# Feed forwards in passes of 8, 8 and 6 inner tiles, with the down projections by seven products of quarters

## The chip, the cores and the metric

The kernel runs on one core of a Trainium2 chip. The metric is the time of one execution in device microseconds; the figure for a kernel is the median of several executions. The engines of the core that matter here are TensorE (PE, with its weight loads as PEld), VectorE (DVE), ScalarE (ACT), GpSimd (POOL) and SyncE (SP); SP issues most of the transfers, and POOL issues those that add to what lies in the target. In this kernel each engine has one stream of instructions, whose order is fixed when the kernel is built.

## The reference, cut to what matters

A trunk of two layers for 512 tokens of width 1024, in f32. Layer 0 mixes with a gated delta rule, layer 1 with sliding window attention; both also attend to 256 memory tokens. Behind the mixer stands in each layer the feed forward, with an inner width of 2816:

```python
def swiglu(h, w_gate_up, w_down):
    gu = h @ w_gate_up
    return (jax.nn.silu(gu[..., :D_FF]) * gu[..., D_FF:]) @ w_down
...
        x = x + jnp.concatenate([mix_out.astype(x.dtype), mem_o.astype(x.dtype)], axis=-1) @ w_out[layer]
        x = x + swiglu(rms_norm(x, ln_ffn[layer]), w_gate_up[layer], w_down[layer])
...
    return rms_norm(x, ln_final)
```

Layer 1 rotates queries and keys by tables of cosines and sines of the positions (the rope tables).

## The kernel before

Activations lie transposed: a tile holds 128 features by 512 tokens, so the residual x is 8 tiles and the inner layer is 22. Every product runs as three matmuls (`mm3`): each operand is split into a high part, a copy by ACT (names `whi`, `h`, `Tah`), and a low part, a subtraction by DVE (`wlo`, `l`, `Tal`), and high by high, high by low and low by high are added up in PSUM. So every weight and every activation costs one ACT copy and one DVE subtraction (`split`, L168). Weights come from memory by SP's transfers into `wraw` and `ws`.

The feed forward (`ffn`, L1099) runs in two halves of 11 inner tiles each: first the gate and up projections of the half, then the half's share of all 8 rows of the down projection. Of the gate and up projections, a few are direct (8 weight tiles by three matmuls, 512 tokens wide, in the PSUM tiles `pj`). The rest go in pairs of output tiles by `quarters` (L1275): the input is cut in two halves of features and two of tokens, the weights of the pair likewise, and seven products of quarters replace the eight of the plain way, as in Strassen's method. Each product is 4 weight tiles by three matmuls, 256 tokens wide, in the PSUM tiles `g`. Sums of weights are made by POOL's accumulating transfers into `ws` and by DVE in `wraw`; sums of the input's quarters (`token_sums`) are made once in a layer. DVE joins the products from PSUM (`fu`, `fg`), and three of them are held for it by ACT copies (`fs`). Six places for split weights (`ring`) go round.

The down projections are direct: for each of 8 rows 11 weight tiles, split as pieces 768 and 640 wide, by three matmuls of 512 tokens. In layer 1 the last two rows run in halves of the tokens, so that the final norm and the store of the first half begin before the second half is done. Behind the first down row of layer 0 stands `rope_tables`: two tens of small DVE steps that depend on each other, all on one tile `ws` and one tile `fu`, with two sines on ACT. Behind layer 0's feed forward the next layer (`swa`) splits x twice by two gains, once for its queries and once for keys and values (`h`, `l` from `x`), and then projects the queries.

The order on each engine comes from the framework's scheduler, which sets the instructions by the order in the code, by priorities and by its own estimates of when operands are there; the code adds a few ordering edges (`nosync`).

Of the kernel before, what the change touches and what calls it, by code (L numbers as in the profile page):

```python
# [9 lines left out]
F32 = mybir.dt.float32  # L10
F32R = mybir.dt.float32r
# [7 lines left out]
P = 128  # L19
# [67 lines left out]
class Builder:  # L87
# [158 lines left out]
    def build(self):  # L246
        tc, nc, a = self.tc, self.nc, self.a
        with ExitStack() as st:
            opened = lambda name, **kw: tc.tile_pool(name=name, bufs=1, reuse_waits="tile", **kw)
            pool = lambda name, **kw: st.enter_context(opened(name, **kw))  # L250
            cp = pool("const")
            self.wpool, self.apool = pool("w"), pool("acta")
            self.dpool = pool("scratch", space=DRAM)
            self.load_constants(cp)
            self.weng = nc.vector
            with opened("layer0", side="right") as self.mpool:
                with self.banks(pj=3, g=2, sc=3):
                    with opened("early", side="right") as ep:
                        self.mem_and_norm(ep)
                    with opened("gdn", side="right") as gp:  # L260
                        mix = self.gdn(gp)
                    self.bpool, xp = pool("actb"), pool("x")
                    self.x = [self.t(xp, [P, T], F32, f"x{k}") for k in range(KD)]
                    for k in range(KD):
                        nc.sync.dma_start(self.x[k], a["xT"][:, k, :])
                    self.rstd, self.cosT, self.sinT = (self.t(xp, [P, T], F32, n) for n in ("rstd", "cosT", "sinT"))
                    h = self.output(xp, 0, mix)
            with opened("ffn0", side="right") as fp, self.banks(pj=2, g=6):
                self.ffn(fp, xp, 0, h, self.apool, rope=True)
            with self.banks(pj=2, qk=2, pt=2), opened("swa", side="right") as sp:  # L270
                h = self.output(xp, 1, *self.swa(sp))
            with opened("ffn1", side="right") as fp, self.banks(pj=2, g=6):
                self.ffn(fp, xp, 1, h, self.bpool)
# [825 lines left out]
    def ffn(self, fp, xp, layer, h, apool, rope=False):  # L1099
# [3 lines left out]
        half = FT // 2  # L1103
        acts, sums, open_pairs, places, waiting, shift, sized = [], [], [], [], [], [0], []

        col = lambda f, up: a["wgu"][layer, 2 * f + up]

        def gate(f, up=()):
            ps = self.project(col(f, 0), h, "pj")
            if f == 0:  # L1110
                list(zip(range(2), up))
                self.rstd_from(acc, *(self.t(fp, [P, T], F32R, "ws", 4) for _ in range(2)), after=self.last,
                               root=(self.cosT, self.sinT) if layer else None)
                self.use(SILU_SIN)
            g = self.t(fp, [P, T], F32, "fg", 4)
            self.tt(nc.vector, g, ps, self.rstd, ALU.mult)
            if f == 2:
                waiting.append(g)
            else:
                self.fn(g, g, AF.Silu)  # L1120
            return g

        def put(u):
            n = len(acts)
            if n == FT // 2 - 1 and not sized:
                sized.append(self.t(fp, [P, 40], F32, "rest"))
            acts.append(self.pair(apool) if n < KD else self.pair(fp, f"ac{n}"))
            self.split(u, *acts[-1])
# [10 lines left out]
        def begin(f, up, by, tag, bufs, then):  # L1139

            o = [self.t(fp, [P, T], F32, tag, bufs) for _ in range(2)]
            steps = self.quarters(fp, [col(f + i, up) for i in range(2)], sums, by, o, ring)
            shift[0] = P - 8
            next(steps)
            while waiting:
                x = waiting.pop()
                self.nosync(self.fn(x, x, AF.Silu), self.held)
            end()
            next(steps)
            open_pairs.append((steps, then, o))  # L1150
            return o

        def end():
            if open_pairs:
                steps, then, o = open_pairs.pop()
                next(steps, None)
                for x in o:
                    then(x)

        def add(x, ps):  # L1160
            d = ps
            if not layer:
                d = self.t(fp, [P, T], F32, "fu", 3)
                self.tt(nc.vector, d, ps, self.rstd, ALU.mult)
            self.tt(nc.vector, x, d, x, ALU.add)

        for f0 in (0, half):
            acts.clear()
            places.clear()
            up = self.projected(col(f0, 1), h, "g")  # L1170
            g = gate(f0, up)
            u = self.t(fp, [P, T], F32, "fu", 3)
            self.tt(nc.vector, u, list(up)[-1], g, ALU.mult)
            put(u)
            for f in range(f0 + 1, f0 + half, 2):
                if f == 1:
                    g = []
                    for i in range(2):
                        for _ in range(2 - i):
                            sums.append(self.token_sums(fp, layer, len(sums), h))  # L1180
                        g.append(gate(f + i))
                    sums.append(self.token_sums(fp, layer, len(sums), h))
                else:
                    g = begin(f, 0, (self.rstd, self.rstd), "fg", 4, lambda x: self.fn(x, x, AF.Silu))
                begin(f, 1, g, "fu", 3, put)
            end()
            self.acc = self.floor if layer else None
            tail = KD - 2 if f0 and layer else KD
            down = lambda m, j, n, **kw: self.weight(a["wdn"][layer, m][:, (f0 + j) * P:(f0 + j + n) * P], **kw)
            for m in range(tail):  # L1190
                if layer and f0 == 0:
                    self.tt(nc.vector, self.x[m], self.x[m], self.root, ALU.mult)
                ps = self.bank("pj")
                for j, n in ((0, 6), (6, 5)):
                    w = down(m, j, n)
                    for k in range(n):
                        self.mm3(ps, w, k, acts[j + k], j + k == 0, j + k == half - 1)
                add(self.x[m], ps)
                if f0:
                    self.acc = self.accumulate(xp, self.acc, self.x[m], m)  # L1200
                if rope and f0 == 0 and m == 0:
                    self.rope_tables(fp)
        if tail < KD:

            parts = (slice(0, T // 2), slice(T // 2, T))
            own = dict(pool=fp, tags=("T", "T"), bufs=8)
            w = {m: [down(m, j, n, **(own if m == KD - 1 else {})) for j, n in ((0, 6), (6, 5))] for m in range(tail, KD)}
# [5 lines left out]
            for t in parts:  # L1213
                acc = self.acc[:, t]
                for m in range(tail, KD):
# [4 lines left out]
                    for k in range(half):  # L1220
                        act = [part[:, t] for part in acts[k]]
                        self.mm3(ps, w[m][k // 6], k % 6, act, k == 0 and not seeded, k == half - 1, seeded)
                    if seeded:
                        x = ps
                    else:
                        add(x, ps)
# [8 lines left out]
            for n, (end, o) in enumerate(zip(ends, outs)):  # L1235
                self.store(*end, o, n)
# [9 lines left out]
    def token_sums(self, fp, layer, j, h):  # L1246
# [9 lines left out]
        c = self.t(fp, [P, q], F32, "fc")  # L1256
        raws = [self.t(fp, [P, T], F32, f"ac{8 + j % 3}{n}") for n in "hl"]
# [17 lines left out]
    def quarters(self, fp, src, sums, by, u, ring):  # L1275
# [3 lines left out]
        (a11, a12), (a21, a22) = ([c[:, :T], c[:, T:]] for c in src)  # L1279
        a1 = self.load(src[0])  # L1280
        s1, s3 = (self.t(fp, [P, T], F32, "ws", 4) for _ in range(2))
# [6 lines left out]
        last = self.t(fp, [P, T], F32, "wraw", 2)  # L1288
# [5 lines left out]
        def product(ps, raw, b, first):  # L1294

            w = ring()
            self.split(raw, *w)
            for j in range(4):
                self.mm3(ps, w, j, sums[j][b], first and j == 0, j == 3, not first)
# [6 lines left out]
        product(pa, a1[:, :T], "11", True)  # L1306
# [6 lines left out]
        self.tt(nc.vector, a1[:, :T], s1, a1[:, :T], ALU.add)  # L1313
        product(pa, a1[:, :T], "t2", False)
        u2 = held(pa)
        product(pb, a1[:, T:], "21", True)
        self.tt(nc.vector, u[0][:, :q], pb, p1, ALU.add)
        self.tt(nc.vector, a1[:, T:], a1[:, :T], a1[:, T:], ALU.add)
        product(pc, a1[:, T:], "22", False)
        self.tt(nc.vector, u[0][:, q:], pc, u2, ALU.add)  # L1320
        self.tt(nc.vector, u[0], u[0], by[0], ALU.mult)
        product(pa, s3, "t3", False)
        self.stt(u[1][:, q:], pa, -1.0, p5, ALU.mult, ALU.subtract)
        self.tt(nc.vector, u[1][:, q:], u[1][:, q:], by[1][:, q:], ALU.mult)
        yield
        product(pa, last, "t4", False)
        self.stt(u[1][:, :q], pa, -1.0, by[1][:, :q], ALU.mult, ALU.mult)
# [227 lines left out]
def layout(i):  # L1555
# [25 lines left out]
    gu = f("w_gate_up")  # L1581
    pair = [j for t in range(FT) for j in (t, FT + t)]
# [3 lines left out]
    for k in range(0, KD, 2):  # L1586
# [10 lines left out]
        "wdn": np.stack([tiles(w) for w in f("w_down")]),  # L1597
# [20 lines left out]
```

## Time and profile before

| what | value |
|---|---|
| time, median of 3 executions | 1130.86 us (1130.72 to 1131.07) |
| the profiled execution: span from first to last instruction | 1129.4 us |
| mean granted TensorE clock of the profiled execution | 0.998 |
| PE busy | 1119.9 us, 99% of the span |
| PEld busy | 986.1 us, 87% |
| DVE busy | 827.6 us, 73% |
| ACT busy | 634.4 us, 56% |
| POOL busy | 73.2 us, 6% |
| mean traffic | 134 GB/s |

The profiled execution is known by its span alone; the median lies 1.5 us above it, which is what stands around the first and the last instruction. The table reads so: the engine with the largest share is PE, and the chain of work that ended last runs through it. The busy share of DVE is a mean over stages of different kinds and has to be read stage by stage.

### The profile page before, as it was taken

Reading aid. Unit: us, or ns where it says so; the run is one execution under the profiler, and the core shown is the slowest. Engines: PE = TensorE matmul, PEld = TensorE weight load, DVE = VectorE, ACT = ScalarE, POOL = GpSimd, SP = SyncE. Lnnn points to the kernel's source line nnn. Section 1 sums busy time; section 2 is a strip of 40 time slices with the busy share of each in tenths; the row PEclk is TensorE's granted clock in tenths of the full one; section 3 lists DMA queues with packets and bytes.
Section 4 is the critical chain, followed back from the end, with each engine's and each line's share of the span. In section 5 each row is a group of like instructions: output and inputs, shape, how many; then the busy total and the mean of one; then the engine's idle time right before and its main releaser. Section 6 shows DMA issues by size and latency. Waiting matters only on the chain.

```text
span 1129.4 us, 19330 instructions
## 1 busy us (share of the span) xinstructions
PE 1119.9 (99%) x7339; PEld 986.1 (87%) x7339; DVE 827.6 (73%) x1553; ACT 634.4 (56%) x1285; POOL 73.2 (6%) x91
## 2 busy tenths in 40 slices
PE   9999999999999999999999999999999999999997
PEld 8888778887899988899988887788999988999986
DVE  7676976577888975588955877839999634889643
ACT  8588664456566632366643555856666422666434
POOL 0000000000021001011000000000111000111001
PEclk9999999999999999999999999999999999999999
DMA  8344252234567536377533321116687533776232
GB/s 314 109 153 149 95 131 86 85 113 145 174 167 195 143 111 169 102 191 195 134 89 102 132 75 38 53 43 180 158 201 185 144 103 105 173 190 156 77 103 87
DMA packets 72401, 151.15 MB, mean 134 GB/s; under 512 B 16956, under 2 KB 18516, under 8 KB 72308
## 3 DMA queue, kind: packets, MB, share of 16 engines
q1 hardware_dynamic: 60884, 129.21, 36.3%
q0 software_dynamic: 11136, 20.45, 11.2%
q8 instruction: 57, 0.93, 0.3%
q14 instruction: 36, 0.29, 0.1%
q10 hardware_dynamic: 288, 0.26, 0.1%
HBM read 142.94 MB, written 6.96 MB: 133 GB/s over the span
## 4 chain that ended last, share of the span: by engine, by line
PE 96%; DVE 2%; ACT 1%; DMA 0%; issue 0%; DVEq 0%; SPq 0%; ACTq 0%
PE pj L146 46%; PE g L146 38%; PE sc L146 6%; PE qk L146 3%; PE pt L146 2%; PE pt L150 1%; PE g L150 1%; DVE big L153 1%; DVE qv L156 0%; DVE btmp L153 0%; DMA early<-in_early 0%; DVE wlo L153 0%; ACT sm L134 0%; DVE T L153 0%; DVE gcr L153 0%
## 5 line engine op out<-in xcount | busy, mean ns | idle before, releaser
L140 ACT ACTIVATE whi<-wraw 128x512 fp32r<-128x512 f32 (+3 forms) x318 | 235.3, 748 | 240.6 <-PE pj L146 164.0
L153 DVE TENSOR_TENSOR wlo<-wraw,whi 128x512 fp32r<-128x512 f32 (+3 forms) x318 | 262.8, 837 | 92.7 <-ACT whi L140 85.2
L146 PE MATMUL pj<-h,whi 128*128 128x512 f32 (+1 forms) x652 | 256.4, 395 | 0.0
L146 PE MATMUL pj<-l,whi 128*128 128x512 f32 (+1 forms) x652 | 254.4, 390 | 0.0
L146 PE MATMUL pj<-h,wlo 128*128 128x512 f32 (+1 forms) x652 | 254.0, 390 | 0.0
L146 PE MATMUL g<-T,whi 128*128 128x256 f32 x1216 | 216.8, 279 | 0.0
L146 PEld LDWEIGHTS g<-T,whi 128*128 128x128 f32 x1216 | 185.1, 188 | 1.3 <-DVE fu L156 1.3
L146 PE MATMUL g<-T,wlo 128*128 128x256 f32 x608 | 169.7, 279 | 0.0
L146 PEld LDWEIGHTS pj<-h,whi 128*128 128x128 f32 x652 | 122.4, 188 | 28.0 <-issue 4.1
L146 PEld LDWEIGHTS pj<-h,wlo 128*128 128x128 f32 x652 | 122.5, 188 | 25.4 <-issue 0.9
L146 PE MATMUL g<-l,whi 128*128 128x256 f32 (+1 forms) x500 | 144.5, 289 | 0.0
L146 PE MATMUL g<-h,whi 128*128 128x256 f32 (+1 forms) x500 | 144.4, 289 | 0.0
L146 PE MATMUL g<-h,wlo 128*128 128x256 f32 (+1 forms) x500 | 144.4, 289 | 0.0
L146 PEld LDWEIGHTS pj<-l,whi 128*128 128x128 f32 x652 | 122.6, 188 | 23.6 <-DVE l L1468 0.3
L146 PEld LDWEIGHTS g<-T,wlo 128*128 128x128 f32 x608 | 114.3, 188 | 0.0
L146 PEld LDWEIGHTS g<-h,whi 128*128 128x128 f32 x500 | 94.0, 188 | 1.9
L146 PEld LDWEIGHTS g<-l,whi 128*128 128x128 f32 x500 | 93.9, 188 | 1.9
L146 PEld LDWEIGHTS g<-h,wlo 128*128 128x128 f32 x500 | 93.9, 188 | 1.8
L1286 POOL DMA_DIRECT2D ws<-in_wgu x38 | 33.5, 881 | 733.0 <-DMA ws<-in_wgu 399.1
L140 ACT ACTIVATE whi<-ws 128x512 fp32r<-128x512 f32 x76 | 48.0, 631 | 42.0 <-PE g L146 35.6
L153 DVE TENSOR_TENSOR wlo<-ws,whi 128x512 fp32r<-128x512 f32 x76 | 52.0, 684 | 5.9 <-ACT whi L140 5.9
L1287 POOL DMA_DIRECT2D ws<-in_wgu x38 | 34.2, 900 | 196.4 <-DVE wlo L153 71.4
(421 smaller groups left out, 1683.2 us busy)
## 6 DMA issues: line engine op xcount, KB each, us to landing
wraw<-in_wgu SPq DMA_DIRECT2D x50, 512.0 KB, 4.4
ws<-in_wgu SPq DMA_DIRECT2D x76, 256.0 KB, 3.4
ws<-in_wgu POOLq DMA_DIRECT2D x76, 256.0 KB, 4.5
wraw<-in_win SPq DMA_DIRECT2D x26, 512.0 KB, 3.6
wraw<-in_wdn SPq DMA_DIRECT2D x32, 384.0 KB, 3.1
wraw<-in_wdn SPq DMA_DIRECT2D x32, 320.0 KB, 2.9
wraw<-in_wgu SPq DMA_DIRECT2D x38, 256.0 KB, 4.0
wraw<-in_wout SPq DMA_DIRECT2D x16, 512.0 KB, 3.6
```

The costliest lines, as they stand in the source:

```text
L140: self.copied = self.nc.scalar.activation(out, in_, AF.Copy, **kw).ins
L146: return self.nc.tensor.matmul(out, lhsT, rhs, start=start, stop=stop, skip_group_check=more).ins
L150: return self.nc.tensor.transpose(out, in_, self.ident[:k, :k]).ins
L153: return eng.tensor_tensor(out=out, in0=a, in1=b, op=op).ins
L1286: nc.gpsimd.dma_start(s1, a22, accum_op=ALU.add)
L1287: nc.gpsimd.dma_start(s3, a21, accum_op=ALU.add)
```

## The change

`ffn8` takes the place of `ffn` in both layers. It does these things:

- It works in three passes of 8, 8 and 6 inner tiles. Only the first two inner tiles of a layer are projected directly; all others go in pairs by `quarters`, whose core is now the shared function `sevens`.
- The down projections go by seven products too: rows in pairs, over the 8 (or 6) tiles of the pass. With 8 tiles a quarter is 4 weight tiles (512 wide), with 6 tiles 3 (384 wide). In the last pass only rows 0 to 5 go in pairs; rows 6 and 7 stay direct with 6 tiles, in layer 1 in halves of the tokens as before.
- For this the inputs of the down projection need sums of token halves: `act_sums` makes them on DVE for each pair of inner tiles (`tmp`), and splits them (`Ta`, `Tb`) beside the inner tiles themselves.
- The rows of the down weights are laid out in another order for this, and the size of the memory kept for POOL's transfer descriptors is set to 2048 (`dynamic_dma_scratch_size`).
- `rope_tables` stands behind the first pair of down rows of layer 0 in the code.

The core of the diff:

```diff
-    def ffn(self, fp, xp, layer, h, apool, rope=False):
+    def ffn8(self, fp, xp, layer, h, apool, rope=False):
...
+        def act_sums(keep):
+            parts, tmp, old = {}, self.t(fp, [P, 3 * q], F32, "tmp"), len(sums)
...
+            def mid(o):
+                u0, u1 = o
+                self.tt(nc.vector, tmp[:, q:2 * q], u1[:, q:], u0[:, q:], ALU.subtract)
...
+                self.tt(nc.vector, u0[:, q:], u0[:, :q], u0[:, q:], ALU.subtract)
+                if keep:
+                    self.split(u0[:, q:], *parts["t1"])
+                else:
+                    self.split(u0, *a0)
+                self.stt(tmp[:, :q], u1[:, q:], -1.0, u0[:, q:], ALU.mult, ALU.subtract)
...
+                self.split(tmp[:, :2 * q], *ta)
+                self.split(u1[:, q:], *parts["22"])
+
+            def fin(o):
+                u1 = o[1]
+                self.split(u1[:, :q], *parts["21"])
+                self.stt(tmp[:, 2 * q:], u1[:, :q], -1.0, tmp[:, :q], ALU.mult, ALU.subtract)
+                parts["t4"] = [self.t(fp, [P, q], F32R, f"Tb{n}", 4) for n in "hl"]
+                self.split(tmp[:, 2 * q:], *parts["t4"])
...
+            def second(pc, u2):
+                self.tt(nc.vector, d[0][:, q:], pc, u2, ALU.add)
+                if not layer:
+                    self.tt(nc.vector, d[0], d[0], self.rstd, ALU.mult)
+                self.tt(nc.vector, x[0], d[0], x[0], ALU.add)
...
+        for size in (8, 8, 6):
...
+            while f < f0 + size:
+                g = columns(f, 0, (self.rstd, self.rstd), ("fg", 4), lambda o: None, silu)
+                columns(f, 1, g, ("fu", 3), *act_sums(keep))
+                f += 2
+            self.acc = self.floor if layer else None
+            for m in range(0, tail, 2):
...
+                rows(m)
+                if rope and f0 + m == 0:
+                    self.rope_tables(fp)
...
+        if not layer:
+            for m in range(tail, KD):
+                w, ps = down(m), self.bank("pj")
+                for n, k in enumerate(order):
+                    self.mm3(ps, w, n, acts[k], n == 0, n == size - 1)
...
+    def sevens(self, fp, src, sums, ring, first, second, third, fourth):
...
-    nc = bacc.Bacc("TRN2", target_bir_lowering=False, num_devices=1)
+    nc = bacc.Bacc("TRN2", target_bir_lowering=False, num_devices=1, dynamic_dma_scratch_size=2048)
```

What the change moves is seen best in the order of the engines at two places.

The first is VectorE at the rope tables, in the down projection of layer 0. `ws` on the left is the tile of angles and `fu` its helper; `wlo` are low parts of split weights. Before:

```order
L153 TENSOR_TENSOR wlo_4559<-wraw_4556,whi_4558 128x768
...
L153 TENSOR_TENSOR wlo_4583<-wraw_4580,whi_4582 128x640
L153 TENSOR_TENSOR fu_4523<-pj_4477,rstd_2743 128x512
L160 TENSOR_SCALAR fu_4529<-ws_4528 128x512
L153 TENSOR_TENSOR x_519_2727<-fu_4523,x_519_2727 128x512
L160 TENSOR_SCALAR fu_4529<-fu_4529 128x512
L153 TENSOR_TENSOR wlo_4608<-wraw_4605,whi_4607 128x768
L156 SCALAR_TENSOR_TENSOR ws_4528<-fu_4529,ws_4528 128x512 x3
L153 TENSOR_TENSOR wlo_4632<-wraw_4629,whi_4631 128x640
L156 SCALAR_TENSOR_TENSOR ws_4528<-fu_4529,ws_4528 128x512 x2
```

And now (`g_4130` is the PSUM tile of the seventh product of rows 0 and 1, `ws_4287` the sum of weights for the second product of rows 2 and 3):

```order
L156 SCALAR_TENSOR_TENSOR fu_4119<-g_4130,rstd_2743 128x256
L156 SCALAR_TENSOR_TENSOR ws_4256<-fu_4257,ws_4256 128x512
L153 TENSOR_TENSOR x_520_2728<-fu_4119,x_520_2728 128x256
L156 SCALAR_TENSOR_TENSOR ws_4256<-fu_4257,ws_4256 128x512 x3
L160 TENSOR_SCALAR fu_4257<-ws_4256 128x512
L160 TENSOR_SCALAR fu_4257<-fu_4257 128x512
L156 SCALAR_TENSOR_TENSOR ws_4256<-fu_4257,ws_4256 128x512 x5
L160 TENSOR_SCALAR ws_4256<-ws_4256 128x512
...
L153 TENSOR_TENSOR ws_4256<-ws_4256,fu_4257 128x512
L160 TENSOR_SCALAR ws_4256<-ws_4256 128x512
L153 TENSOR_TENSOR wraw_4285<-ws_4287,wraw_4285 128x512
L153 TENSOR_TENSOR wlo_3313<-ws_4287,whi_3312 128x512
```

Splits of weights stood between the steps of the rope tables; now all steps that stand behind the evacuation of the seventh product (`fu_4119<-g_4130`) come ahead of the next split (`wlo_3313`). The three rows left out are steps of the tables as well, the first of them `sinT` from the first sine.

ScalarE at the same place, now: `ws_4275` and `cosT_2744` are the two sines, `whi` the high parts.

```order
L140 ACTIVATE fs_4312<-g_4295 128x256
L134 ACTIVATE ws_4275<-ws_4256 128x512
L134 ACTIVATE cosT_2744<-ws_4256 128x512
L140 ACTIVATE whi_3312<-ws_4287 128x512
L140 ACTIVATE whi_3314<-wraw_4285 128x512
L140 ACTIVATE whi_3312<-ws_4288 128x512
L140 ACTIVATE whi_3314<-ws_4417 128x512
L140 ACTIVATE whi_3316<-wraw_4285 128x512
```

Both sines stand ahead of the high part of `ws_4287`, for the second product of rows 2 and 3; a high part for rows 4 and 5 (from `ws_4417`, which takes the place in memory that the angles had) stands ahead of one for rows 2 and 3 (the last row shown, for their fifth product). TensorE, now, at the end of rows 0 and 1:

```order
L146 MATMUL g_4130<-Tbh_4183,whi_3314 128x256
L146 MATMUL g_4130<-Tbl_4184,whi_3314 128x256
L146 MATMUL g_4130<-Tbh_4183,wlo_3315 128x256
L146 MATMUL g_4297<-h_3276,whi_3312 128x256
L146 MATMUL g_4297<-l_3277,whi_3312 128x256
L146 MATMUL g_4296<-h_3284,whi_3316 128x256
L146 MATMUL g_4297<-h_3276,wlo_3313 128x256
```

Behind the last matmul of the seventh product (the third row) the next one already takes `whi_3312`, the high part of `ws_4287` that ScalarE makes behind both sines.

The second place is VectorE at the end of layer 0's feed forward, where `l<-x,gains,h` are the splits of x for layer 1 and `wlo ... 128x1024` belongs to its queries; `x_526` is the last tile of x. Before, from the second but last row of the down projection on:

```order
L153 TENSOR_TENSOR x_525_2733<-fu_6657,x_525_2733 128x512
L153 TENSOR_TENSOR wlo_6796<-wraw_6793,whi_6795 128x1024
L156 SCALAR_TENSOR_TENSOR l_6730<-x_519_2727,gains_67,h_6729 128x512
L153 TENSOR_TENSOR sqa_6662<-sqa_6609,sq_6660 128x512
L156 SCALAR_TENSOR_TENSOR l_6734<-x_520_2728,gains_67,h_6733 128x512
```

And now, from the evacuation of the last row on:

```order
L153 TENSOR_TENSOR fu_7597<-pj_7578,rstd_2743 128x512
L156 SCALAR_TENSOR_TENSOR l_7633<-x_523_2731,gains_67,h_7632 128x512
L153 TENSOR_TENSOR x_526_2734<-fu_7597,x_526_2734 128x512
L156 SCALAR_TENSOR_TENSOR l_7637<-x_524_2732,gains_67,h_7636 128x512
L156 SCALAR_TENSOR_TENSOR l_7641<-x_525_2733,gains_67,h_7640 128x512
L153 TENSOR_TENSOR sqa_7602<-sqa_7570,sq_7600 128x512
L156 SCALAR_TENSOR_TENSOR l_7645<-x_526_2734,gains_67,h_7644 128x512
L156 SCALAR_TENSOR_TENSOR l_7649<-x_519_2727,gains_67,h_7648 128x512
...
L156 SCALAR_TENSOR_TENSOR l_7677<-x_526_2734,gains_67,h_7676 128x512
L153 TENSOR_TENSOR wlo_7683<-wraw_7680,whi_7682 128x1024
```

The last split of x that is shown ahead of the row of dots and the one behind it are the first and last of eight for keys and values, one for each tile of x. The low part of the first query weight stood ahead of the splits of x; now it stands behind all of them. TensorE takes it in its fifth matmul behind the last down row:

```order
L146 MATMUL pj_7578<-h_7163,wlo_7575 128x512
L146 MATMUL pj_7686<-h_7616,whi_7682 128x512
L146 MATMUL pj_7686<-l_7617,whi_7682 128x512
L146 MATMUL pj_7717<-h_7616,whi_7713 128x512
L146 MATMUL pj_7717<-l_7617,whi_7713 128x512
L146 MATMUL pj_7686<-h_7616,wlo_7683 128x512
```

The four matmuls ahead of the last row need high parts only.

More of the change, by code (lines that the diff above doesn't have):

```diff
@@ L1097, in output @@
         return h
-    def ffn(self, fp, xp, layer, h, apool, rope=False):
+    def ffn8(self, fp, xp, layer, h, apool, rope=False):
         nc, a = self.nc, self.a
         acc = self.acc
-        half = FT // 2
-        acts, sums, open_pairs, places, waiting, shift, sized = [], [], [], [], [], [0], []
+        q = T // 2
+        hsums, open_pairs, places, shift = [], [], [], [0]
         col = lambda f, up: a["wgu"][layer, 2 * f + up]
[L1108 to L1128, printed above, removed]
         def ring():
@@ new lines, in gate @@
+        def gate(f):
+            ps = self.project(col(f, 0), h, "pj")
+            if f == 0:
+                list(zip(range(2), ups[0]))
+                self.rstd_from(acc, *(self.t(fp, [P, T], F32R, "ws", 4) for _ in range(2)), after=self.last,
+                               root=(self.cosT, self.sinT) if layer else None)
+                self.use(SILU_SIN)
+            g = self.t(fp, [P, T], F32, "fg", 4)
+            self.tt(nc.vector, g, ps, self.rstd, ALU.mult)
+            self.fn(g, g, AF.Silu)
+            return g
@@ L1167, in ffn @@
[L1167 to L1202, printed above, removed]
@@ L1292, in quarters, with product @@
         pa, pb, pc = (self.bank("g")[:, :q] for _ in range(3))
[L1294 to L1299, printed above, removed]
+        def product(ps, raw, b, begin):
+            hl = [x[:, :w] for x in ring()]
+            self.split(raw, *hl)
+            for j, parts in enumerate(sums):
+                self.mm3(ps, hl, j, parts[b], begin and j == 0, j == len(sums) - 1, not begin)
         def held(ps):
```

165 lines of the change are left out of this document (122 added, 43 removed).

## The prediction

> **What bounds the kernel now.** First the page: the span, the shares of the engines, and the chain that ended last.
>
> ```profile
> span 1129.4 us, 19330 instructions
> PE 1119.9 (99%) x7339; PEld 986.1 (87%) x7339; DVE 827.6 (73%) x1553; ACT 634.4 (56%) x1285; POOL 73.2 (6%) x91
> PE 96%; DVE 2%; ACT 1%; DMA 0%; issue 0%; DVEq 0%; SPq 0%; ACTq 0%
> ```
>
> PE is busy throughout and is the chain. A matmul less is time saved, as long as nothing else comes late. Next the pieces of the chain in order of time (start, length, what), cut to the feed forwards: `g` are 256 wide matmuls of the products of quarters, `pj` 512 wide direct ones.
>
> ```profile
> 307.64 10.89 PE pj L146 x48
> 318.53 86.80 PE g L146 x744
> 407.51 64.65 PE pj L146 x285
> 472.16 102.05 PE g L146 x852
> 577.04 65.59 PE pj L146 x289
> 1060.08 51.66 PE pj L146 x259
> ```
>
> 86.80 us over 744 is 0.1167 us for a 256 wide matmul, 10.89 over 48 is 0.2269 us for a 512 wide one. PE runs without a gap through both halves of layer 0. Third, the other engines stage by stage (from:to, length, then busy time of PE, PEld, DVE, ACT, POOL with counts, clock, DMA share, GB/s):
>
> ```profile
> 318.50:407.50 89.00, 89.00 (x761) 88.70 (x760) 79.03 (x143) 55.45 (x106) 12.22 (x14) 1.00 0.66 166
> 407.50:472.20 64.70, 64.70 (x287) 53.53 (x286) 37.89 (x59) 16.14 (x22) 3.68 (x4) 1.00 0.51 142
> 577.00:643.00 66.00, 66.00 (x293) 54.54 (x292) 43.28 (x59) 30.27 (x44) 0.00 (x0) 1.00 0.35 107
> 1123.00:1126.00 3.00, 0.00 (x0) 0.00 (x0) 1.51 (x4) 0.02 (x1) 0.78 (x2) 0.62 0.73 258
> 1126.00:1130.00 4.00, 0.00 (x0) 0.00 (x0) 0.00 (x0) 0.00 (x0) 0.00 (x0) 0.50 0.20 71
> ```
>
> The 73% of DVE is a mean of two unlike stages: 89% in gate and up (79.03 of 89.00), 59% and 66% in the down rows. The change fills the second and adds to the first. The last two rows show PE idle at the end: the granted clock falls to 0.62 and 0.50.
>
> **What PE saves.** A gate and up pair by products is 84 matmuls of 0.1167, 9.80 us, against 48 of 0.2269, 10.89 directly; each layer has one more such pair: 1.09. Down rows of a layer before: 8 x 22 x 3 x 0.2268 (64.65 over 285) = 119.8. After: eight pairs of rows over 8 tiles at 9.80 = 78.4, three over 6 tiles at 63 x 0.1167 = 7.35, together 22.1, and two direct rows of 18 x 0.2268, 8.2; sum 108.6, saving 11.1. In layer 1 the two token-halved rows shrink from 132 to 72 matmuls of 0.1167, saving 0.2 more. Both layers: 12.2 + 12.4 = **24.6 us off PE**.
>
> **What DVE pays.** Prices, grouped by shape (count, busy, mean ns, idle before):
>
> ```profile
> L153 DVE TENSOR_TENSOR wlo<-wraw,whi 128x512 fp32r<-128x512 f32 x190 | 127.6, 688 | 16.9 <-ACT whi L140 12.1
> L153 DVE TENSOR_TENSOR fu<-g,fs 128x256 f32<-128x256 f32 x40 | 16.9, 423 | 11.1 <-PE g L146 9.7
> L140 ACT ACTIVATE whi<-ws 128x512 fp32r<-128x512 f32 x76 | 48.0, 631 | 42.0 <-PE g L146 35.6 <-ACT fs L140 6.4
> ```
>
> Neighbours overlap a little. The rows of DVE in time around the rope tables (start, length) give the step from start to start:
>
> ```profile
> 414.40 0.69 DVE L153 TENSOR_TENSOR fu<-pj,rstd 128x512 f32<-128x512 f32 x1 [1.98 <-PE pj L146]
> 415.00 0.42 DVE L160 TENSOR_SCALAR fu<-ws 128x512 f32<-128x512 f32 x1
> 415.34 0.69 DVE L153 TENSOR_TENSOR x<-fu,x 128x512 f32<-128x512 f32 x1
> ...
> 417.14 2.14 DVE L156 SCALAR_TENSOR_TENSOR ws<-fu,ws 128x512 f32<-128x512 f32 x3
> 419.20 0.82 DVE L153 TENSOR_TENSOR wlo<-wraw,whi 128x640 fp32r<-128x640 f32 x1
> ...
> 421.38 0.43 DVE L160 TENSOR_SCALAR fu<-ws 128x512 f32<-128x512 f32 x1
> 421.84 0.43 DVE L160 TENSOR_SCALAR fu<-fu 128x512 f32<-128x512 f32 x1
> ...
> 429.36 0.49 DVE L160 TENSOR_SCALAR sinT<-ws,consts 128x512 f32<-128x512 f32 x1 [0.70 <-ACT ws L134]
> ...
> 433.11 0.42 DVE L160 TENSOR_SCALAR ws<-ws 128x512 f32<-128x512 f32 x1
> ```
>
> So 0.60 for a 512 wide tensor operation (414.40 to 415.00), 0.34 for one of 0.42 (415.00 to 415.34), which I take for the 256 wide ones too, and 0.71 for each of a dependent chain (2.14 over 3). A gate and up iteration (19.60 us of PE) now has 14 splits, 4 weight sums, 2 evacuations and 2 activation operations of 0.60, and 17 of 256 at 0.34: 22 x 0.60 + 17 x 0.34 = 19.0; waits inside `act_sums` add perhaps 0.3. Before it was 16.6 by the same count (21 x 0.60 + 12 x 0.34). That is 97 to 98% of PE: hidden, just, by DVE's lead, up to five products (7 us) in a ring of six. A down pair in layer 0 is 9 weight operations and 3 evacuations 512 wide and 5 of 256, 8.9 of 9.80: hidden. In the last pass nine of 384 at about 0.47 (between 0.34 and 0.60), two sums of squares and the same evacuations also make 8.9, now against 7.35: three pairs fall behind by 4.7, of which the lead takes some; I take **3**, bounds 0 and 4.7. Layer 1 needs no factor rstd: 1 there; x times the root falls into the first pass, eight of 0.60: 1.5, bounds 0 and 4.8; and the token halves at the end have less PE work to lie beside: 2. Together **5** for layer 1, bounds 0 and 8. ACT has room: four more copies in an iteration, 2 us at 0.63 or less, on 55.45 of 89.00. Transfers: the down weights come as 512 KB and five pieces of 256 KB where 704 KB came a row, with POOL's additions; the rows of issues below are the price where one lies on the path. The smaller memory for descriptors I cost at nothing: even if each of a pair's two additions waited for the one ahead to land (4.5 below), that is 9 of the pair's 9.80.
>
> **Rope tables.** Before, the splits stood between the chain's steps, and PE waited for nothing. Now DVE evacuates the seventh product of rows 0 and 1, and can only do that once PE has finished it; the rest of the chain follows without a split, and on ACT both sines stand ahead of the high part that PE's next matmul takes. So from the end of that product PE waits for: evacuation and the add to x, 2 x 0.42; nine chained operations, 9 x 0.71 = 6.4; three single ones at 0.46 (421.38 to 421.84), 1.4; the sine's wait, 0.70; four single ones and an add, 2.5; the second sine and the high part, 0.63 each. That is 13.1, and the low part's 0.69 less two matmuls of 0.12 makes **13.5**. Bounds: 0 if the chain had run before, which the evacuation in front excludes for all but the first step; 19 is what it took between splits (415.00 to 433.53). On SP's queue the load of `ws` for that product stands behind the positions and three weight loads that wait for earlier splits; hidden, as the chain is longer. Next, a high part for rows 4 and 5 stands on ACT ahead of one that rows 2 and 3 need; its `ws` place comes free only with the second sine:
>
> ```profile
> ws<-in_wgu SPq DMA_DIRECT2D x76, 256.0 KB, 3.4
> ws<-in_wgu POOLq DMA_DIRECT2D x76, 256.0 KB, 4.5
> ```
>
> Load and addition, 7.9, with the copies on both sides 9.2 after the sine; PE has 0.6 of waiting and three products of 1.40 in that time: **4.4**, bounds 2 and 6.
>
> **From layer 0 to layer 1.** Before, these rows:
>
> ```profile
> 629.08 0.69 DVE L153 TENSOR_TENSOR x<-fu,x 128x512 f32<-128x512 f32 x1
> 629.69 1.22 DVE L153 TENSOR_TENSOR wlo<-wraw,whi 128x1024 fp32r<-128x1024 f32 x1
> 630.82 0.74 DVE L156 SCALAR_TENSOR_TENSOR l<-x,gains,h 128x512 fp32r<-128x512 f32 x1
> ...
> 632.09 4.06 DVE L156 SCALAR_TENSOR_TENSOR l<-x,gains,h 128x512 fp32r<-128x512 f32 x6
> ```
>
> The query weight was split ahead of the splits of x. Now DVE has, from the end of the last down row: evacuation 0.69, add 0.60, four splits of x and a sum of squares, 4 x 0.66 (4.06 over 6, with the overlap) + 0.60, then eight splits for keys and values, 5.3, and the weight, 1.22: 11.0. PE has four matmuls, 0.9: **10.1**. Bounds: 4.8 if the eight splits stood behind, which the order excludes, and 13 if ACT's copies beside them are late.
>
> **Clock.** PE idles at three places for 4 to 13 us. The rows at 1123 and 1126 show the clock down after that; no row shows how fast it returns. If the return takes as long as the fall, the 3 us of the first of those rows, half speed costs 1.5 at each of three places: bounds 0 and 4.5. I take **2**, since only the longest of the three idles for much longer than those rows span.
> The Trainium skill, "TensorE: Matmul & The Clock Gate", Part 1, states half speed for the first 3.4 us or so of work after an idle window of that length; by it each of the three would cost 1.7, 5 in all, and the sum would be 1147. The fall agrees with the rows here; the return is shown by none.
>
> **Sum.** Span 1129.4 and 1.5 around it, 1130.9, which is the median: 1130.9 - 24.6 + 13.5 + 4.4 + 10.1 + 3 + 5 + 2 = **1144**, 1.2% slower. With all but the two chains at their lower bounds it is 1132 (13.5 + 2 + 10.1), with all at their upper 1162 (19 + 6 + 13 + 4.7 + 8 + 4.5).
>
> All of it rests on DVE and ACT doing their rows strictly in the order built. That a weight's split waits for PE before is in the rows (`whi<-ws`, 35.6 us idle for `g`), and no row shows a later instruction of one engine overtaking.
> The Trainium skill, "Perfetto Trace Analysis", Tensor Engine Instruction, says that ACT and DVE are strict FIFO, while PE may pull weight loads ahead; if they were not, the sum would be the first rival's.
>
> **The rivals.**
> - *The saving comes through* (faster). The stalls at both places are hidden, because DVE and ACT run far ahead of PE there and the evacuation isn't the end of PE's lead. Then 1130.9 - 24.6 + 3 + 5 = 1114, at best 1106. It decides once the stalls together are under 16 us. For it: PE without a gap in 407 to 643 before, and DVE at 59%. Against: both orders have a row that needs PE's last result ahead of one that PE waits for. 0.13.
> - *One of the two places only* costs its full price: 1130.9 - 24.6 + 8 + 10 to 18 is 1124 to 1132. For it: the two places have nothing in common but the order. Against: the same order shows both. 0.12.
> - *DVE becomes the bound of every gate and up pair.* If an operation costs 0.63 where I take 0.60, or 0.37 for 0.34, an iteration is 20.2 to 20.5; with 20 iterations and the lead used up once in a pass, 10 more: 1154. For it: 79.03 of 89.00 busy already, and 97% leaves nothing for a wait. Against: 16.9 us of idle before 190 splits, so waits were few. 0.19.
> - My forecast, 1137 to 1151: 0.56.
>
> Slower by over 0.2% (some 2 us, what a measurement of this kernel tells from none): 0.56 + 0.19 and 0.01 of the second rival, 0.76; within: 0.06 of the second; faster: 0.13 + 0.05, 0.18. Range 1120 to 1158: it leaves out the first rival's most and the worst of the third.
>
> **What would show it.** Right: a PE gap near 13 us behind the first pair of down rows of layer 0, ended by ACT's `whi<-ws`, with a second of some 4 behind it; one near 10 ahead of the queries, ended by `wlo`; 0.1167 still per 256 wide matmul; `g` in layer 0's gate and up without gaps; clock under 1 behind the gaps. Wrong: gaps of PE spread over all gate and up stretches with DVE near 100% (third rival), or both places closed (first). What I know least is the clock's return and DVE's lead when it runs at 97%.

## The result, and the profile after

The changed kernel takes 1157.06 us (median of 4, 1156.9 to 1157.86) against 1130.79 us beside it: the ratio is 1.0231 (95% interval 1.022 to 1.0243), 26 us slower. The forecast had the way and the two main places, and 13 of the 26 us. The time lies outside its 1137 to 1151.

The page of the profile after: the span, the shares, the busy tenths of PE, DVE and the clock in 40 slices, and the chain.

```profile
span 1155.1 us, 21831 instructions
PE 1113.6 (96%) x8119; PEld 1014.6 (88%) x8119; DVE 981.9 (85%) x1999; ACT 721.7 (62%) x1537; POOL 115.3 (10%) x139
PE   9999999999999599999999699999999999999996
DVE  7676967577899989999999867848999889998995
PEclk9999999999999899999999899999999999999999
PE 78%; DVE 17%; ACT 3%; issue 2%; DMA 0%; DVEq 0%; ACTq 0%
```

PE had 99% of a shorter span; it has 96% of a longer one, with two holes (the 5 and the first 6 in its row; the last 6 is the end), and the clock falls in the same two slices. DVE holds 17% of the chain, where it held 2%. Who waited for whom, PE's rows (total, times, longest):

```profile
PE g L146 <- ACT whi L140: 14.6, 3, 13.0
PE pj L146 <- DVE wlo L153: 8.6, 1, 8.6
PE pj L146 <- ACT whi L140: 2.4, 2, 1.6
```

These are the two places of the forecast. PE's matmuls in time there show what they waited for (start, length, and the idle time ahead in brackets):

```profile
389.43 0.28 PE L146 MATMUL g<-Tbh,wlo 128*128 128x256 f32 x1
402.66 0.58 PE L146 MATMUL g<-h,whi 128*128 128x256 f32 x1 [12.95 <-ACT whi L140]
...
648.40 0.39 PE L146 MATMUL pj<-l,whi 128*128 128x512 f32 x1
650.37 0.50 PE L146 MATMUL pj<-h,whi 128*128 128x512 f32 x1 [1.58 <-ACT whi L140]
650.71 0.40 PE L146 MATMUL pj<-l,whi 128*128 128x512 f32 x1
659.72 0.79 PE L146 MATMUL pj<-h,wlo 128*128 128x512 f32 x1 [8.62 <-DVE wlo L153]
```

The first is the end of the seventh product of down rows 0 and 1 and the second product of rows 2 and 3 behind the rope tables; the other is the first two queries of layer 1. VectorE's rows in the same stretches name what stood in between:

```profile
389.83 0.42 DVE L156 SCALAR_TENSOR_TENSOR fu<-g,rstd 128x256 f32<-128x256 f32 x1
391.10 2.14 DVE L156 SCALAR_TENSOR_TENSOR ws<-fu,ws 128x512 f32<-128x512 f32 x3
394.20 3.60 DVE L156 SCALAR_TENSOR_TENSOR ws<-fu,ws 128x512 f32<-128x512 f32 x5
402.64 0.69 DVE L153 TENSOR_TENSOR wlo<-ws,whi 128x512 fp32r<-128x512 f32 x1 [0.61 <-ACT whi L140]
...
652.48 6.05 DVE L156 SCALAR_TENSOR_TENSOR l<-x,gains,h 128x512 fp32r<-128x512 f32 x9
658.44 2.36 DVE L153 TENSOR_TENSOR wlo<-wraw,whi 128x1024 fp32r<-128x1024 f32 x2
```

VectorE is busy nearly without a pause in both gaps; most of it is work that nobody waits for yet.

Stages, with the clock before the DMA share, as in the table of before: a stretch of gate and up in layer 0, the work behind the first gap (twice, cut at two ends), behind the second, and a short stretch in layer 1.

```profile
420.00:475.00 55.00, 55.00 (x469) 55.00 (x469) 51.92 (x104) 31.96 (x65) 9.62 (x11) 1.00 0.77 191
403.00:408.00 5.00, 5.00 (x24) 4.99 (x24) 2.14 (x4) 0.65 (x2) 1.43 (x2) 0.50 0.91 202
403.00:409.50 6.50, 6.50 (x36) 6.49 (x35) 2.40 (x5) 2.10 (x5) 2.19 (x3) 0.58 0.90 197
660.00:665.00 5.00, 5.00 (x14) 3.90 (x15) 1.41 (x2) 0.00 (x0) 0.00 (x0) 0.56 0.64 209
893.20:896.40 3.20, 3.14 (x14) 3.14 (x15) 1.81 (x4) 1.44 (x5) 0.00 (x0) 0.50 0.69 151
```

The first row answers the third rival: 469 matmuls in 55.00 us are 0.117 each, so PE lost nothing there, with VectorE at 94%. The others show the granted clock at 0.50: behind the first gap 24 matmuls of 256 take 5.00 us, 0.21 each. The mean of 0.58 up to 409.50 puts the return at 408.4 (half speed for 5.4 of the 6.5 us), that of 0.56 up to 665 at 664.4.

To sort the whole loss I took all start times of matmuls in the two feed forwards and the queries behind the first, and added up what each step (the time from the start of one matmul to the start of the next) had above 0.1166 us (256 wide) or 0.2268 us (512 wide). Before, that is 1.0 us in layer 0 and 2.0 in layer 1; after, 37.5 and 14.6. So 36.5 + 12.6 - 24.6 saved = 24.5 us, of the 25.7 by which the spans differ. The counts of matmuls in the two traces (3709 of 256 wide and 2580 of 512 before, 5539 and 1530 after) give 24.8 saved at these two prices. The terms stand in the section behind the experiments.

### The profile page after: what moved, and what is told of

It is laid out like the page before. It is cut to its first block, busy times and chain, and to the rows that moved or that the text cites. A ratio compares the mean times of both kernels' runs of the same rounds, so it can differ in the third digit from the quotient of the medians.

```text
span 1155.1 us, 21831 instructions
## 1 busy us (share of the span) xinstructions
PE 1113.6 (96%) x8119; PEld 1014.6 (88%) x8119; DVE 981.9 (85%) x1999; ACT 721.7 (62%) x1537; POOL 115.3 (10%) x139
## 3 DMA queue, kind: packets, MB, share of 16 engines
q1 hardware_dynamic: 65492, 135.11, 36.5%
## 4 chain that ended last, share of the span: by engine, by line
PE 78%; DVE 17%; ACT 3%; issue 2%; DMA 0%; DVEq 0%; ACTq 0%
PE g L146 46%; PE pj L146 21%; PE sc L146 6%; DVE wlo L153 5%; PE qk L146 3%; DVE fu L153 2%; PE pt L146 1%; PE pt L150 1%; DVE x L153 1%; DVE l L156 1%; DVE wraw L153 1%; DVE sqa L153 1%; PE g L150 1%; ACT whi L140 1%; DVE ws L156 1%
## 5 line engine op out<-in xcount | busy, mean ns | idle before, releaser
L146 PE MATMUL g<-h,whi 128*128 128x256 f32 (+1 forms) x852 | 244.7, 289 | 15.9 <-ACT whi L140 13.0
L146 PE MATMUL g<-l,whi 128*128 128x256 f32 (+1 forms) x852 | 243.0, 287 | 0.0
L146 PE MATMUL g<-h,wlo 128*128 128x256 f32 (+1 forms) x852 | 242.0, 286 | 0.0
L146 PEld LDWEIGHTS g<-l,whi 128*128 128x128 f32 x852 | 160.8, 189 | 1.9
L146 PE MATMUL pj<-h,wlo 128*128 128x512 f32 (+1 forms) x388 | 152.6, 395 | 8.6 <-DVE wlo L153 8.6
L146 PE MATMUL pj<-h,whi 128*128 128x512 f32 (+1 forms) x388 | 155.1, 403 | 2.4 <-ACT whi L140 2.4
L146 PE MATMUL pj<-l,whi 128*128 128x512 f32 (+1 forms) x388 | 152.8, 394 | 0.0
L140 ACT ACTIVATE whi<-ws 128x512 fp32r<-128x512 f32 (+1 forms) x124 | 76.4, 616 | 67.0 <-PE g L146 58.1
L153 DVE TENSOR_TENSOR wlo<-ws,whi 128x512 fp32r<-128x512 f32 (+1 forms) x124 | 83.6, 674 | 3.0 <-ACT whi L140 3.0
L140 ACT ACTIVATE fs<-g 128x256 f32<-128x256 f32 x186 | 67.6, 366 | 3.3 <-PE g L146 3.0
```

The source lines that it names most:

```text
L140: self.copied = self.nc.scalar.activation(out, in_, AF.Copy, **kw).ins
L146: return self.nc.tensor.matmul(out, lhsT, rhs, start=start, stop=stop, skip_group_check=more).ins
L153: return eng.tensor_tensor(out=out, in0=a, in1=b, op=op).ins
```

## The experiments

All times below are medians beside a kernel before of 1131.0 to 1131.1 us; ratios are to that one.

| run | median us | ratio, 95% interval |
|---|---|---|
| passes in layer 0 only | 1156.77 | 1.023 (1.0213 to 1.0247) |
| passes in layer 1 only | 1130.29 | 0.9995 (0.9986 to 1.0004) |
| rope chain early | 1143.58 | 1.0103 (1.0088 to 1.0118) |
| query weights first | 1148.37 | 1.0152 (1.0137 to 1.0167) |
| both of these | 1134.01 | 1.0025 (1.0014 to 1.0037) |
| layer 1 only, root on GpSimd | 1138.08 | 1.0062 (1.0049 to 1.0075) |
| layer 1 only, tail | 1128.42 | 0.9976 (0.9967 to 0.9985) |
| both, root on GpSimd, tail | 1137.69 | 1.006 (1.0047 to 1.0073) |
| layer 1 only, tail, root tied | 1125.95 | 0.9953 (0.994 to 0.9965) |
| both, tail, root tied | 1128.72 | 0.9979 (0.997 to 0.9988) |
| and layer 0's last pass direct | 1121.36 | 0.9921 (0.9907 to 0.9934) |
| and layer 1's last pass direct | 1117.91 | 0.9891 (0.9875 to 0.9908) |

### One layer at a time

The old `ffn` is called in one layer, `ffn8` in the other, and the down weights are laid out for each.

```diff
-                self.ffn8(fp, xp, 1, h, self.bpool)
+                self.ffn(fp, xp, 1, h, self.bpool)
```

> Layer 0 with the passes of 8, 8 and 6, layer 1 with the feed forward of before. Theory (the loss sits in layer 0, at the rope tables and ahead of the queries, as the trace after shows it: 13.1 us and 3.2 of slow clock, 10.5 and 2.4, and some 7 elsewhere, against 12.2 saved): 1130.8 - 12.2 + 36.5 = 1155, that is nearly all of the slowdown. Rival (VectorE's load, which both layers share alike, makes the loss): half of it, 1144.

> Layer 0 with the feed forward of before, layer 1 with the passes. Theory: what layer 1 loses (12.6 us more than before by the matmuls' start times) just eats the 12.4 it saves: 1131 to 1132, no difference that could be told. Rival (VectorE's load in both layers alike): 1144.

1156.77 and 1130.29: layer 0 alone is as slow as both, and layer 1 alone is as fast as before. The rival, a load that both layers share alike, is out.

### The two stalls

The rope chain leaves the feed forward, and works on tiles that wait for their use anyway:

```diff
+                    self.rope_angles()
...
+        r, n = self.sinT, self.cosT
+        nc.sync.dma_start(n.bitcast(I32), a["positions"].partition_broadcast(P))
...
+    def rope_tables(self, pool):
+        self.fn(self.sinT, self.sinT, AF.Sin)
+        self.fn(self.cosT, self.cosT, AF.Sin)
```

> The changed kernel with the rope tables' chain of VectorE steps moved ahead of the feed forward, beside the output projection of layer 0, on the tables' own tiles; only the two sines stay behind the first pair of down rows. The result is the same. Theory: the gap of 13.1 us, the slow clock behind it (3.2) and the 0.4 go: 1157.1 - 16.7 = 1140, or 1143 if the chain costs some of it in the output projection. Rival (the feed forward of layer 0 is bound by VectorE anyhow, and the gap only moves): 1152 or more.

1143.58, 13.5 us less. The wait for `whi` shrank from 14.6 to 1.7, and the other one stayed, as two rows of PE's waits show:

```profile
PE pj L146 <- DVE wlo L153: 8.3, 1, 8.3
...
PE g L146 <- ACT whi L140: 1.7, 2, 1.5
```

Where the chain now is it costs something: by the matmuls' start times 2.7 us are lost at 310 to 330 us, at the start of the feed forward, where the change loses nothing. The profiled execution took 1140.29 us, the least of the four (the others 1143.4 to 1143.8); its trace also lacks the half speed that the change's trace shows in layer 1, which this edit doesn't touch. So the steps of this edit are known to within 2 or 3 us only.

The second edit changes only the order:

```diff
+        first = {t: self.weight(a["wq"][t]) for t in (6, 7)}
...
+        splits(h, G_MIX[1], self.apool)
...
         list(beside7)
+        splits(hk, G_KV, self.bpool)
```

> The changed kernel with the first two query weights of layer 1 set ahead of the splits of x in the code, and the splits for keys and values behind these two queries. Theory: of the gap of 10.5 us about 2.4 stays, since the third to eighth split of x still follow the last down row, and the slow clock of 2.4 goes: 1157.1 - 10.5 = 1146.5. Rival (the splits for keys and values are only late next, ahead of the keys): 1152 or more.

1148.37, 8.7 us less than the change, where 10.5 was expected. The longest wait of the queries fell from 8.6 to 2.2, a stretch of 3.4 us at half speed is left (634.4 to 637.8 in its trace), and the rope's wait is untouched:

```profile
PE g L146 <- ACT whi L140: 14.6, 3, 13.0
...
PE pj L146 <- DVE wlo L153: 2.2, 1, 2.2
```

> The rope chain ahead of the feed forward and the query weights ahead of the splits of x, both in the changed kernel. Theory (two stalls with nothing in common but the built order): the gains add, 13.5 + 8.7: 1157.1 - 22.2 = 1135, still slower than before by 4, the rest being the last rows of both layers and layer 1's first pass. Rival (the one gap hides part of the other's work): 1139 or more.

1134.01: the gains add (13.5 + 8.7 = 22.2; measured 23.1). The two stalls add up as independent ones do, and with them mostly gone the change is 3 us from before.

### What layer 1 loses

Three edits were tried on the kernel with passes in layer 1 alone, whose saving of 12.4 us leaves nothing. The first gives the eight products of x with the root (which stands in `cosT` there) to GpSimd.

```diff
-                        self.tt(nc.vector, self.x[i], self.x[i], self.root, ALU.mult)
+                        self.tt(nc.gpsimd, self.x[i], self.x[i], self.root, ALU.mult)
```

> The kernel with the passes in layer 1 alone (1130.3), with the eight products of x and the root, which VectorE does in layer 1's first pass, given to GpSimd. Theory (VectorE is at its limit in that pass, and these 8 x 0.60 us are what PE lost there, 2.6 us and 1.7 of slow clock): 1130.3 - 2.5 to 4 = 1126 to 1128. Rival (the loss there comes from the handovers between ScalarE and VectorE in the sums of activations): no change, 1130.

1138.08, 7.8 us slower: both expectations missed. The timeline of GpSimd and VectorE shows why. Eight products run on GpSimd at 793 to 808, and VectorE's instructions stretch while they do:

```profile
793.64 1.62 POOL L153 TENSOR_TENSOR x<-x,cosT 128x512 f32<-128x512 f32 x1
795.50 3.17 POOL L153 TENSOR_TENSOR x<-x,cosT 128x512 f32<-128x512 f32 x2
800.57 7.68 POOL L153 TENSOR_TENSOR x<-x,cosT 128x512 f32<-128x512 f32 x5 [1.90 <-DVE Tah L156]
```

```profile
793.51 5.72 DVE L153 TENSOR_TENSOR T<-Tal,T 128x512 fp32r<-128x512 f32 x1
800.42 0.47 DVE L156 SCALAR_TENSOR_TENSOR Tal<-x,gains,Tbh 128x256 f32<-128x256 f32 x1
800.81 1.50 DVE L156 SCALAR_TENSOR_TENSOR Tah<-x,minus,Tah 128x256 f32<-128x256 f32 x1
802.24 1.78 DVE L153 TENSOR_TENSOR wlo<-ws,whi 128x512 fp32r<-128x512 f32 x1
...
807.04 0.68 DVE L153 TENSOR_TENSOR fg<-pj,rstd 128x512 f32<-128x512 f32 x1
```

A subtraction of 0.68 us takes 5.72, a split 1.78, a step of 0.47 takes 1.50; the last row, with one operand from PSUM, keeps its 0.68. By the matmuls' start times TensorE loses some 9.7 us more at 800 to 820 than without the edit, part of it at half speed (the granted clock is 0.50 from 807.2 to 817.4, with PE busy for 5.35 of the 10.20 us), and 2 us less at 860 to 880, where the products had stood on VectorE. So the theory's loss went away, and a larger one came. The second edit, called the tail, splits the last row's weight early and orders ScalarE's copies by when x is done:

```diff
+            if keep and layer and m == 0:
+                last.append(self.weight(a["wdn"][layer, KD - 1][:, f0 * P:], pool=fp, tags=("T", "T"), bufs=8))
...
-            for o, t in zip(outs, parts):
-                for k in range(tail):
+            for k in range(tail):
+                for o, t in zip(outs, parts):
                     self.put_row(o, k, self.x[k][:, t])
```

> The kernel with the passes in layer 1 alone (1130.3), with the last row's down weight split ahead of the last pass's rows, and ScalarE's copies of x into the output tiles in the order in which x is done. Theory (the 6.5 us that the end of layer 1 loses are waits for these two): 1130.3 - 3 to 5 = 1125 to 1127. Rival (the last pass is bound by VectorE, 8.9 us a pair against 7.35, and these edits only move work within it): 1129.5 or more.

1128.42, 1.9 us less, between the two expectations. By the matmuls' start times the end (1100 to 1120) loses 2.2 us in place of 6.6, and the last pass (1080 to 1100) 4.8 in place of 1.7: the waits were there, but most of what they gave back is lost again in the last pass, which is the rival's mechanism.

> All four edits in the changed kernel. Theory: 1135 less 2.5 to 4 less 3 to 5: 1126 to 1129.5, faster than before by 0.1 to 0.4%. Rival (VectorE at 97% takes back what one edit gives): 1131 or more.

1137.69, slower than both expectations: 1134.0 less the tail's 1.9 and with GpSimd's 7.8 on top would be 1139.9. The same VectorE instructions stretch in its trace (5.48, 1.51, 1.78 us).

The products with the root go back to VectorE, but behind the first evacuation of the down rows that need them:

```diff
             def first(pb, p1):
-                self.tt(nc.vector, d[0][:, :q], pb, p1, ALU.add)
+                ins = self.tt(nc.vector, d[0][:, :q], pb, p1, ALU.add)
+                if scaled:
+                    for y in x:
+                        self.nosync(self.tt(nc.vector, y, y, self.root, ALU.mult), ins)
```

> Passes in layer 1 alone, with the tail's edit (1128.4) and the eight products of x and the root kept on VectorE, but tied behind the first evacuation of the pair of down rows that needs them, out of the gate and up stretch. Theory (VectorE at its limit in layer 1's first gate and up iterations made the 2.6 us there): 1128.4 - 2.5 = 1126. Rival (the handovers of the sums of activations make it): no change, 1128.4.

1125.95, 2.5 us less, as the theory had it. The same stretch of the first pass with the products in it (first row, from the kernel with passes in layer 1 alone; with the tail the same three waits of 0.8 us come 2 us later) and behind the edit (second row):

```profile
861.00:867.00 6.00, 4.16 (x32) 3.55 (x30) 6.00 (x14) 3.92 (x9) 0.87 (x1) 1.00 0.66 198
```

```profile
861.00:867.00 6.00, 5.75 (x47) 5.35 (x46) 5.92 (x13) 4.22 (x11) 0.87 (x1) 1.00 0.81 215
```

VectorE was full, and PE did 32 matmuls in six us; without the products in that place it did 47.

### A version that beats both

> The changed kernel with the rope chain early, the query weights first, the tail's edit and the products with the root tied to the down rows. Theory: 1134.0 - 2 - 2.6 - 1.7 (slow clock behind the gap) = 1128, faster than before by 0.25%. Rival: as for the kernel with layer 1 alone, 1132.

1128.72: 0.21% faster than before, near the 1128 expected.

```diff
+            if keep and not layer:
+                def put(o):
+                    for u in o:
+                        acts.append(self.pair(apool))
+                        self.split(u, *acts[-1])
+                return put_none, put
...
-            tail = KD - 2 if keep else KD
+            plain = keep and not layer
+            tail = 0 if plain else KD - 2 if keep else KD
```

> As the one before, but in layer 0 the last pass is direct in all eight rows, without sums of activations. Theory (that pass is bound by VectorE, 8.9 us a pair against 7.35, and its delay reaches into layer 1's queries): TensorE pays 3 x 0.82 = 2.5 and gets back 3.7 in the pass and 2 to 4 at the queries: 1128 - 1 to 5 = 1123 to 1127. Rival (the products' saving outweighs the wait): 1129 or more.

1121.36, 7.4 us less although PE has 2.5 us more to do, and below the 1123 to 1127 expected: in this pass, three pairs by products of 6 tiles, with the sums of activations that they need, cost more than they save on PE. By the matmuls' start times the pass loses 0.2 us in place of 4.9, and the queries behind it (up to 671 in both traces) 2.3 in place of 6.2, a half speed stretch of 3.4 us included. The same in layer 1:

> As the one before, but the last pass is direct in layer 1 too. Theory: TensorE pays 2.5 and gets back what that pass loses there, 3.1 + 1.5 + some 1 by the matmuls' start times: 1121.4 - 1 to 3 = 1118.5 to 1120.5. Rival (the loss there is the end's own handovers, which stay): 1124.

1117.91, a little below the range expected and 1.1% faster than before (0.9891, 0.9875 to 0.9908). Its shares, from its page:

```profile
span 1115.6 us, 21257 instructions
PE 1104.1 (99%) x7957; PEld 1000.6 (90%) x7957; DVE 944.9 (85%) x1882; ACT 700.0 (63%) x1465; POOL 105.0 (9%) x127
```

PE is at 99% again: of the 24.6 us that the change takes off PE, less 4.9 for two direct last passes, 13.2 arrive. Of the rest 2.7 are lost at 310 to 330 us, behind the rope chain's new place.

## Why the prediction was right, and where its sizes were off

By the matmuls' start times in the change (removal in an experiment beside it, where there was one):

| step of the prediction | predicted us | measured us | removed by an edit |
|---|---|---|---|
| PE saves | 24.6 | 24.8 by the count of matmuls | |
| rope tables, gap | 13.5 | 13.1 | 13.5 with its slow clock |
| high part for rows 4 and 5 | 4.4 | 0.4 | |
| layer 0 to layer 1 | 10.1 | 10.5 | 8.7 with its slow clock |
| last pass of layer 0 | 3 | 3.7 | |
| clock | 2 | 3.2 + 2.4 + 1.7 | |
| layer 1 | 5 | 10.9 without its 1.7 of clock | 1.9 + 2.5 |
| rest of layer 0, not forecast | 0 | 3.2 | |

- **The total** was half right: the way and the mechanism are the forecast's, the size isn't. 1157.06 lies nearer to the third rival's 1154 than to 1144, and it is within the range of 1120 to 1158 only by the room left for that rival, which the trace refutes. That the range holds is luck. What the sum lacked is mostly layer 1 (5.9), the clock (5.3) and the rest of layer 0 (3.2), with 4.0 too much for the high part.
- **PE's saving and the two gaps** came as worked out from the built order and rows of before: 13.5 and 10.1 against 13.1 and 10.5. For the queries an edit of the order alone takes 8.7 us away, with the same work on VectorE. For the rope tables the edit takes the chain out of the stretch (13.5 us): it shows that the chain is the gap's cause; that the splits' place behind it makes the gap is read from the trace, and wasn't run by itself.
- **The high part for rows 4 and 5** was sized at 4.4 and cost 0.4. ScalarE did wait for it (4.40 us, for the transfer of `ws`), but the load and addition were there 6.0 us after the second sine, where the forecast had 7.9 (9.2 with the copies), and PE's three products in between ran at half clock and filled that time. The step missed that a slow clock also stretches the cover.
- **The clock** was sized at 2 and cost 7. I let the return take as long as the fall at the end of the kernel; the trace shows half speed for 5.8 us behind the first gap (402.7 to 408.4; 2.9 of the 3.2 in the table, which is all that is lost up to 410), 4.7 behind the second and 3.4 in layer 1. The third place of the forecast, the gap of 4.4, wasn't there, and the one in layer 1 was not forecast: three waits of 0.8 us stood ahead of it. The same three waits (0.7 to 0.8 us) stand in the traces with passes in layer 1 alone and with the rope chain early, and the clock doesn't fall there, so these 1.7 us come and go. The Trainium skill, "TensorE: Matmul & The Clock Gate", Part 1, gives about 3.4 us of half speed to a restart; the clock's term by it was 5 instead of 2, nearer to the 7 measured. The trace agrees on the factor (0.50) and exceeds the length at both gaps.
- **Layer 1** was sized at 5 and lost 10.9, and this is the largest miss. The mechanisms were named, but not their sizes. The products with the root were given 1.5; they lost 2.4 in gaps, and the clock fell behind them in this execution. The end was given 2 and lost some 6.5: the last row's weight and ScalarE's copies came late, and when they come early, VectorE's load in the last pass takes most of that back. The edits give back 1.9 and 2.5; the direct last pass gives 3.5 more (1121.36 to 1117.91).
- **DVE at 97%** as a cover held where I claimed it: PE loses under 1 us in any ten of layer 0's gate and up. The third rival is out as a general bound, and is right where more operations are put into that stretch: the eight products in layer 1's first pass, and the rope chain's new place. Its arithmetic was also loose: 0.63 or 0.37 alone makes an iteration 19.5 to 19.6 us long, and only both together 20.2 to 20.5. The first two rivals are out, since both places cost their price.
- **The last pass of layer 0** cost 3.7 itself, as sized; what I didn't see is that its backlog on VectorE also reaches the queries. The direct pass took 7.4 us off, with 2.5 more work for PE; by the start times above the pass gains 4.7 and the queries 3.9, half speed included.

Not tried: the smaller memory for transfer descriptors by itself. It is in every run above, so its price, if it has one, is open; the run with passes in layer 1 alone, and the fastest one, carry it too.

## What to carry to other kernels

Where instructions are moved, read each in-order engine at the places where one of its rows has to wait for TensorE's last result: whatever stands between that row and the next operand that TensorE needs is a gap at its full price, even on an engine that was 60% busy in that stage before, and the price can be added up beforehand from rows. Add half a clock for some 5 us behind gaps of 9 to 13 us (4.7 and 5.8 here). And a method that trades TensorE's work for VectorE's pays only in stages where VectorE has that much time: here the last passes, with 3 weight tiles a quarter, were better direct, and the passes with 4 are part of a kernel that is 1.1% faster than before.

## What the runs showed of the hardware

- GpSimd's tensor operations can hold VectorE's up. With eight 512 wide products on GpSimd (1.62 us the first, 7.68 the last five), VectorE's neighbours took 1.50 to 1.78 us in place of 0.47 to 0.68, and one 5.72; the kernel lost 7.8 us to save 4.8 of VectorE's time. The Trainium skill, "SBUF — State Buffer", SBUF: two separate sides, states an exclusive lock on a shared pair of ports between the two, held for a whole instruction against VectorE operations with two SBUF inputs. The rows agree: those that stretched have two such inputs, and the one at 807.04, with one input from PSUM, did not stretch.
- The granted clock can fall to 0.50 without a long gap: in the change's layer 1, 1.66 us of idle in six (PE busy 4.34 of 6.00, the row below) went ahead of 3.4 us at half speed. It need not: with passes in layer 1 alone, PE was busy for 4.16 of six (the row 861 to 867 above), with the same three waits of 0.8 us, and the clock stayed at 1.00 up to the end of the kernel. No run here shows what decides between the two.

```profile
887.00:893.00 6.00, 4.34 (x33) 3.73 (x31) 6.00 (x15) 3.73 (x8) 0.88 (x1) 1.00 0.72 214
```
